# Weight splits and the attention half's additions to x move from GpSimd to VectorE in a two-layer hybrid encoder trunk

## The chip, the core and the metric

The kernel runs on one core of a Trainium2 chip. The metric is the time of one execution on the device in microseconds (us). A profile shows the engines of the core: PE (TensorE, matrix products; PEld is its weight load), DVE (VectorE), ACT (ScalarE), POOL (GpSimd) and SP, whose queue issues the DMA transfers. Engines work through their own instruction lists in order and wait for each other by semaphores.

## What is computed

x has 256 tokens of 1024 features. Two layers, each:

```
x += 1/2 SwiGLU_a(RMSNorm(x) * g)                    # D_FF = 2816
u  = (RMSNorm(x) * g) @ W_in                          # the mixer begins
     columns A: neighbourhood attention, 8 heads x 64
     columns B: short convolution, gates, long convolution (FFT), 512 channels
x += ([RMSNorm(y_A) ; RMSNorm(y_B)] * g_out) @ W_out  # the mixer ends
x += 1/2 SwiGLU_b(RMSNorm(x) * g)
x += sigmoid((RMSNorm(x) * g) @ W_g) * (p[i] @ W_p)
```

and a last RMSNorm. All arrays are float32. To keep more bits than one pass of the fast matrix format gives, each operand is split in two: `h`, the rounded copy, and `l`, what is left (`src - h`). A product is then the sum of three: h by h, h by l and l by h.

## The kernel before

All activations are kept transposed: feature on the partition, token (256) along the row, eight tiles `x[0..7]` of 128x256. Weights stream in from memory as pieces `raw` of 128x2048 (1 MB, three buffers). `part()` splits one half of a piece (eight tiles of 128x128, 128x1024 numbers) in two steps: ACT makes `wh` (a cast, L285), and then `wl = raw - wh` is one subtraction (L288). Six halves can be split ahead of use. The variable `Stream.on_pool` decides who does the subtraction: inside the mixer every third half goes to POOL (`ON_POOL = 3`), elsewhere all go to DVE. The last reader of a piece frees its buffer for the next load.

`Fiber`s are generators that are stepped while PE's matmuls are written out, and so they set where side work stands between the matmuls. PE's and ACT's instructions keep the order in which they are written. DVE's, POOL's and SP's are placed by the framework's scheduler.

The order in the mixer (`ORDER`): value columns, then groups of columns for gate (`g`), query and key (`q`), scores (`s`), transposes of the softmax (`t`), attention (`p`), transform of u (`u`, `f`), outer gate (`x`), inverse transform (`i`), and at the end `a0` to `a7`: the attention half of W_out's product, one 128x256 tile of x each. `add(c, ps, st, e)` waits for the row scale of the norm (`rna`), multiplies on DVE (L942) and adds to `x[c]` (L943) on the engine `e`, which is POOL here. Then comes the convolution half of the same product, whose row scale is `rhy`: it multiplies and adds on DVE (L942, L943), and at once `prep` makes the next stage's operand: ACT writes `xg` (L368), DVE its remainder (L370), ACT squares x (L353), POOL sums the squares in `acc` (L356). PE's first products of the next SwiGLU (L191, L200) read `xg`.

Other names in the rows: L426 to L435 are the small instructions of a norm's row scale (`Rstd`), L442 and L443 its broadcast on PE, L444 its copy; L731 to L742 make q and k; L839 and L840 are the side taps of the short convolution; L854 is the gate product `u` on POOL; L779 scales the softmax and L786 transposes it.

Of the kernel before, what the change touches and what calls it, by code (L numbers as in the profile page):

```python
# [49 lines left out]
SPREAD_F = 10  # L50
FILTER = 10
LAG = 0
ON_POOL = 3

# [24 lines left out]
def hybrid_trunk(ctx: ExitStack, tc: tile.TileContext, w, xT, pT, rpb, small, wf, zT, dft, idft, decay, out):  # L81
    nc = tc.nc
    V, S, G, PE = nc.vector, nc.scalar, nc.gpsimd, nc.tensor
# [15 lines left out]
    def nm(s):  # L99
        uid[0] += 1  # L100
        return f"{s}{uid[0]}"

    def bank():
        return psp.tile([P, 512], F32, tag="ps", name=nm("ps"))
# [4 lines left out]
    def t1(dt=F32, s="s"):  # L109
        return k1.tile([P, T], dt, tag="k1", name=nm(s))  # L110
# [4 lines left out]
    def f(ap):  # L115
        return ap.bitcast(F32)
# [31 lines left out]
    def spawn(gen, first=False):  # L148
        fb = Fiber(gen)
        Pace.live.insert(0 if first else len(Pace.live), fb)  # L150
        return fb
# [13 lines left out]
    def rest(n):  # L165
        for _ in range(n):
            yield

    def mm3(o, lh, ll, rh, rl, start, stop):
        PE.matmul(o, lh, rh, start=start, stop=False)  # L170
        PE.matmul(o, lh, rl, start=False, stop=False)  # L171
        PE.matmul(o, ll, rh, start=False, stop=stop)  # L172
        paced(o.free_size() // T if hasattr(o, "free_size") else o.shape[-1] // T)
# [66 lines left out]
    class Stream:  # L240
        loaded = 0
        parted = 0
        used = 0
        on_pool = 0
        raws = {}
        ready = {}

    def load():
        n = Stream.loaded
        if n >= DEPTH * PIECES:  # L250
            return
        raw = rawp.tile([P, 16, P], F32, tag="raw", name=nm("raw"))
        src = w[n].rearrange("p (a b) -> p a b", b=P)
        if n == 0:
            nc.sync.dma_start(sm, small)
            for q in range(4):
                nc.sync.dma_start(raw[:, 4 * q : 4 * q + 4], src[:, 4 * q : 4 * q + 4])
                nc.sync.dma_start(x[q], xT[q])
        elif n == 1:
            for q in range(2):  # L260
                nc.sync.dma_start(x[4 + 2 * q], xT[4 + 2 * q])
                nc.sync.dma_start(raw[:, q * HALF : (q + 1) * HALF], src[:, q * HALF : (q + 1) * HALF])
                nc.sync.dma_start(x[5 + 2 * q], xT[5 + 2 * q])
        else:
            nc.sync.dma_start(raw, src)
        Stream.raws[n] = raw
        Stream.loaded += 1

    def part(steps=1):

        n = Stream.parted
        Stream.parted += 1
        while Stream.loaded < min(n // 2 + 2, DEPTH * PIECES):
            load()
        raw = Stream.raws[n // 2]
        h = whp.tile([P, HALF, P], F32R, tag="wh", name=nm("wh"))
        l = wlp.tile([P, HALF, P], F32R, tag="wl", name=nm("wl"))
        fb = Fiber(None)
        Stream.ready[n] = (h, l, fb)

        def go():
            k = HALF // steps
            for a in range(0, HALF, k):
                src = raw[:, n % 2 * HALF + a : n % 2 * HALF + a + k]
                S.copy(h[:, a : a + k], src)  # L285
                yield
                e = G if Stream.on_pool and n % Stream.on_pool == 0 else V
                e.tensor_sub(l[:, a : a + k], src, f(h[:, a : a + k]))  # L288
            if n % 2:
                Stream.raws.pop(n // 2)  # L290
                load()

        fb.gen = go()
        return fb

    def half():

        n = Stream.used
        Stream.used += 1
        h, l, fb = Stream.ready.pop(n)  # L300
        fb.finish()
        refill(n - LAG)
        return h, l
# [40 lines left out]
    class Squares:  # L344
# [5 lines left out]
        def add(self, src):  # L350
            self.seen += 1
            q = self.ac if self.seen == 1 else t1(s="q")
            S.activation(q, src, AF.Square)  # L353
            last = self.seen == self.n
            if self.seen > 1 and (self.join or not last):
                G.tensor_add(self.ac, self.ac, q)  # L356
            if last:
                self.parts.extend([self.ac] if self.join else [self.ac, q])
# [308 lines left out]
    def mixer(i):  # L667
# [3 lines left out]
        def columns(between=None):  # L671

            b = bank()
            product(b[:, :T], ws, xs)
            if between:
                between()
            product(b[:, T:], ws, xs)
            return b
# [4 lines left out]
        for quarter in range(4):  # L683
            h, l = half()
# [59 lines left out]
        class Head:  # L744
# [7 lines left out]
            def scores(self, st):  # L752
                st.fb.finish()
                b = bank()
                for tt in range(2):
                    qs = slice(T * self.par + tt * P, T * self.par + (tt + 1) * P)
                    mm3(b[:, tt * T : (tt + 1) * T], st.qh[:, qs], st.ql[:, qs], st.kh, st.kl, True, True)
                self.e = t2()
                self.fb = spawn(self.softmax(b), True)
# [21 lines left out]
            def turn(self):  # L781
                self.fb.finish()
                b = bank()
                for kt in range(2):
                    for tt in range(2):
                        PE.transpose(  # L786
                            b[:, kt * T + tt * P : kt * T + (tt + 1) * P],
                            self.e[:, tt * T + kt * P : tt * T + (kt + 1) * P],
                            ident,
                        )  # L790
                self.h, self.l = t2(F32R), t2(F32R)
                self.fb = spawn(self.parts(b), True)
# [6 lines left out]
        yna, yhy = [], []  # L799
# [47 lines left out]
        def gated(c, b):  # L847
            t = t1(s="u")

            def go():  # L850
                res = [t1(), t1()]
                yield from conv(b, (8 + c, 4 + c), res)
                yield
                G.tensor_mul(t, *res)  # L854

            u.append((t, spawn(go())))
# [3 lines left out]
        def outer(c, b):  # L860
            res = [t1(s="x0"), t1(s="x0")]
            fb = spawn(conv(b, (c, c + 1), res))
            x0.extend((r, fb) for r in res)
# [65 lines left out]
        def project(wo, c, parts):  # L929
            ps = bank()[:, :T]  # L930
            for k in range(4):
                wh, wl = wo.next()
                hl, fb = parts[k]
                fb.finish()
                mm3(ps, wh, wl, hl[:, :T], hl[:, T:], k == 0, k == 3)
            return ps

        def add(c, ps, st, e):
            yield from rest(EV)
            yield from st.wait()  # L940
            t = t1()
            V.tensor_mul(t, ps, st.dst)  # L942
            e.tensor_add(x[c], x[c], t)  # L943
# [21 lines left out]
        qs, hs, added, wo = {}, {}, [], Tiles()  # L965
        for kind, j in MIXER:
            if kind == "g":
                gated(j, columns())
            elif kind == "q":
                qs[j] = QK(columns())  # L970
            elif kind == "x":
                outer(2 * j, columns())
            elif kind == "s":
                hs[j] = scores(j, qs.pop(j))
            elif kind == "t":
                turn(hs[j])
            elif kind == "p":
                attend(j, hs.pop(j))
                if len(yna) == 4:
                    na = Rstd(rna, nsq.parts, HY, [fb for _, fb in yna], STAT_NA, SPREAD_NA)  # L980
            elif kind == "u":
                u_turned()
            elif kind == "f":
                forward(j)
            elif kind == "i":
                backward(j)
                if len(yhy) == 4:
                    hy = Rstd(rhy, hsq.parts, HY, [fb for _, fb in yhy], STAT_HY, SPREAD_HY)
            elif kind == "a":
                added.append(spawn(add(j, project(wo, j, yna), na, G)))  # L990
        wo = Tiles()
        new_norm()
        for c in range(KD):
# [9 lines left out]
    def ple_input(i):  # L1003
        pr = t2()
        nc.sync.dma_start(v2(pr), pT[i].rearrange("(a p) t -> p a t", p=P))
        ph, pl = t2(F32R), t2(F32R)

        def go():
            yield from rest(8)
            split(pr, ph, pl)  # L1010

        return ph, pl, spawn(go())
# [88 lines left out]
        Pace.live.append(part())  # L1101
    scaled.extend((hl, Fiber(iter(()))) for hl in hls)
    for i in range(DEPTH):
        Stream.on_pool = 0
        flt = spawn(filter_steps(i))
        ffn(i, C_MIX, i)
        flt.finish()
        Stream.on_pool = ON_POOL
        mixer(i)
        Stream.on_pool = 0  # L1110
        given = ple_input(i)
        ffn(i, C_PLE, i)
        ends, outs = ple(i, i == DEPTH - 1, given)
# [146 lines left out]
```

## Time and profile before

| what | value |
|---|---|
| time, median of 3 runs | 1099.89 us (1099.7 to 1102.32) |
| profiled execution, its own time | 1098.94 us |
| its span, first to last instruction | 1097.2 us |
| PE busy | 1066.1 us (97%) |
| DVE busy | 912.0 us (83%) |
| ACT busy | 649.2 us (59%) |
| POOL busy | 266.1 us (24%) |
| splits of weights on DVE, on POOL (L288) | 328, 22 |
| additions L943 on DVE, on POOL | 16, 16 |
| mean granted clock of PE | 0.994 |

The mixers of the two layers lie at about 203 to 343 us and 732 to 881 us of the span. [...]

### The profile page before, as it was taken

What the parts mean: (1) busy time and instruction counts of PE and PEld (TensorE: products, weight loads), DVE (VectorE), ACT (ScalarE), POOL (GpSimd) and SP (SyncE); (2) the same over time, 40 slices, a digit from 0 to 9 for tenths busy, and PEclk for the clock granted to TensorE, in tenths of its full rate; (3) what the DMA queues carried; (4) which work ended last, traced back from release to release, by engine and by line L of the source; (5) the groups of instructions that cost most, each with busy time, mean ns of one, the idle gap of its engine ahead of it and who ended that gap; (6) DMA issues with size and microseconds to landing.
All of it is one profiled execution on the core that took longest, in us unless ns stands there. A gap on an engine that the chain in (4) does not pass through costs nothing.

```text
span 1097.2 us, 18014 instructions
## 1 busy us (share of the span) xinstructions
PE 1066.1 (97%) x6716; PEld 964.1 (88%) x6716; DVE 912.0 (83%) x1552; ACT 649.2 (59%) x1182; POOL 266.1 (24%) x270
## 2 busy tenths in 40 slices
PE   7989999999998999999999999999999999999995
PEld 6878888899997888888988888889989888888895
DVE  4999987798999988856789999787899998886565
ACT  7566565367746766554666665544856476665444
POOL 3211120534363211100112113025442721110101
PEclk9989999999999999999999999999999999999998
DMA  8556545554425555555465654554622465554621
GB/s 318 199 202 227 192 163 183 177 180 163 154 78 201 196 192 193 188 192 177 169 211 184 231 192 158 188 177 168 194 78 90 151 220 202 192 192 159 208 94 39
DMA packets 32983, 194.07 MB, mean 177 GB/s; under 512 B 3584, under 2 KB 6528, under 8 KB 10880
## 3 DMA queue, kind: packets, MB, share of 16 engines
q1 hardware_dynamic: 32896, 192.92, 51.4%
q8 instruction: 53, 0.87, 0.3%
q14 instruction: 34, 0.28, 0.1%
HBM read 191.86 MB, written 1.05 MB: 176 GB/s over the span
## 4 chain that ended last, share of the span: by engine, by line
PE 79%; DVE 13%; ACT 4%; issue 3%; DMA 0%; POOL 0%; SPq 0%; DVEq 0%; ACTq 0%; POOLq 0%
PE ps L191 41%; PE ps L200 21%; PE ps L171 5%; PE ps L172 5%; PE ps L170 5%; DVE wl L288 3%; ACT wh L285 1%; DVE s L839 1%; DVE rt L399 1%; DVE x L943 1%; DVE s L942 1%; ACT t L779 1%; DVE xg L370 1%; ACT t L772 0%; DVE y L808 0%
## 5 line engine op out<-in xcount | busy, mean ns | idle before, releaser
L288 DVE TENSOR_TENSOR wl<-raw,wh 128x1024 fp32r<-128x1024 f32 (+1 forms) x328 | 405.3, 1258 | 103.2 <-PE ps L200 61.3
L285 ACT CAST wh<-raw 128x1024 fp32r<-128x1024 f32 (+1 forms) x350 | 362.4, 1042 | 157.0 <-PE ps L191 86.1
L191 PE MATMUL ps<-xg,wh 128*128 128x512 f32 x1408 | 347.3, 396 | 12.9 <-DVE xg L1091 6.7
L191 PEld LDWEIGHTS ps<-xg,wh 128*128 128x128 f32 x1408 | 260.0, 191 | 64.7 <-DVE xg L370 8.1
L200 PEld LDWEIGHTS ps<-xg,wl 128*128 128x128 f32 x1408 | 182.1, 191 | 7.7
L200 PE MATMUL ps<-xg,wl 128*128 128x256 f32 x1408 | 184.2, 283 | 0.0
L191 PE MATMUL ps<-act,wh 128*128 128x512 f32 x704 | 173.0, 391 | 0.0
L490 POOL TENSOR_TENSOR gu<-gu,rb 128x256 f32<-128x256 f32 x88 | 69.6, 796 | 394.4 <-DVE gu L208 326.3
L191 PEld LDWEIGHTS ps<-act,wh 128*128 128x128 f32 x704 | 128.3, 189 | 23.9
L356 POOL TENSOR_TENSOR acc<-acc,q 128x256 f32<-128x256 f32 x62 | 55.9, 902 | 295.0 <-ACT q L353 293.8
L170 PE MATMUL ps<-xg,wh 128*128 128x256 f32 x448 | 127.5, 285 | 0.0
L171 PE MATMUL ps<-xg,wh 128*128 128x256 f32 x448 | 126.7, 283 | 0.0
L172 PE MATMUL ps<-xg,wl 128*128 128x256 f32 x448 | 126.7, 283 | 0.0
L200 PEld LDWEIGHTS ps<-act,wl 128*128 128x128 f32 x704 | 92.9, 191 | 5.1
L200 PE MATMUL ps<-act,wl 128*128 128x256 f32 x704 | 94.4, 282 | 0.0
L171 PEld LDWEIGHTS ps<-xg,wh 128*128 128x128 f32 x448 | 85.9, 192 | 0.1
L170 PEld LDWEIGHTS ps<-xg,wh 128*128 128x128 f32 x448 | 85.9, 192 | 0.1
L172 PEld LDWEIGHTS ps<-xg,wl 128*128 128x128 f32 x448 | 85.9, 192 | 0.0
L205 ACT COPY gu<-ps 128x256 f32<-128x256 f32 x176 | 56.2, 374 | 33.1 <-PE ps L200 32.7
L288 POOL TENSOR_TENSOR wl<-raw,wh 128x1024 fp32r<-128x1024 f32 x22 | 56.1, 2550 | 64.0 <-ACT wh L285 51.2
L208 DVE TENSOR_TENSOR gu<-gu,ps 128x256 f32<-128x256 f32 x176 | 66.3, 413 | 0.0
L368 ACT ACTIVATE xg<-x,sm 128x256 fp32r<-128x256 f32 x56 | 28.2, 508 | 59.3 <-DVE x L527 39.9
(196 smaller groups left out, 1386.9 us busy)
## 6 DMA issues: line engine op xcount, KB each, us to landing
raw<-in_w SPq DMA_DIRECT2D x172, 1024.0 KB, 5.0
bias<-in_rpb SPq DMA_DIRECT2D x16, 256.0 KB, 2.9
raw<-in_w SPq DMA_DIRECT2D x4, 256.0 KB, 4.4
x<-in_xT SPq DMA_DIRECT2D x8, 128.0 KB, 5.0
raw<-in_w SPq DMA_DIRECT2D x2, 512.0 KB, 5.5
t<-in_wf SPq DMA_DIRECT2D x4, 256.0 KB, 5.6
dec<-in_decay SPq DMA_DIRECT2D x4, 256.0 KB, 6.3
out<-o SPq DMA_DIRECT2D x4, 256.0 KB, 2.5
```

The lines of the kernel that those rows point to most:

```text
L170: PE.matmul(o, lh, rh, start=start, stop=False)
L171: PE.matmul(o, lh, rl, start=False, stop=False)
L172: PE.matmul(o, ll, rh, start=False, stop=stop)
L191: PE.matmul(b, lh, r, start=start, stop=False)
L200: PE.matmul(o, ll, rh, start=False, stop=stop)
L205: S.copy(dst, b[:, T:])
L208: V.tensor_add(dst, dst, b[:, :T])
L285: S.copy(h[:, a : a + k], src)
L288: e.tensor_sub(l[:, a : a + k], src, f(h[:, a : a + k]))
L356: G.tensor_add(self.ac, self.ac, q)
L368: S.activation(hl[:, :T], x[c], AF.Copy, scale=g)
L490: G.tensor_mul(u, u, rb)
```

## The change

All splits go to DVE, and so do the additions of the attention half to x. POOL's list in the two mixers loses 22 subtractions and 16 additions; DVE's gains the same 38. No instruction of PE, ACT or SP changes its place. DVE's list is placed by the scheduler, so some neighbours of the added rows trade places as well.

```
-ON_POOL = 3
...
-        on_pool = 0
...
                 S.copy(h[:, a : a + k], src)
                 yield
-                e = G if Stream.on_pool and n % Stream.on_pool == 0 else V
-                e.tensor_sub(l[:, a : a + k], src, f(h[:, a : a + k]))
+                V.tensor_sub(l[:, a : a + k], src, f(h[:, a : a + k]))
...
             elif kind == "a":
-                added.append(spawn(add(j, project(wo, j, yna), na, G)))
+                added.append(spawn(add(j, project(wo, j, yna), na, V)))
...
-        Stream.on_pool = 0
         flt = spawn(filter_steps(i))
         ffn(i, C_MIX, i)
         flt.finish()
-        Stream.on_pool = ON_POOL
         mixer(i)
-        Stream.on_pool = 0
```

Line numbers of the changed kernel are lower by three from the subtraction on (L288 is L285 there, L943 is L940).

DVE's list in the first layer's mixer, where the first gate's convolution ends (`s_2455`) and the first q and k (`t_2552`) are made, before:

```order
L839 SCALAR_TENSOR_TENSOR s_2455<-t_2470,sm,s_2455 128x255
L715 TENSOR_TENSOR vl_2353<-t_2474,vh_2349 128x2x64
L840 SCALAR_TENSOR_TENSOR s_2455<-t_2470,sm,s_2455 128x255
L715 TENSOR_TENSOR vl_2353<-t_2474,vh_2349 128x2x64
L731 TENSOR_TENSOR t_2552<-ps_2442,rb 128x512
```

The same place in the changed kernel:

```order
L285 TENSOR_TENSOR wl_2486<-raw_2325,wh_2485 128x1024
L836 SCALAR_TENSOR_TENSOR s_2455<-t_2470,sm,s_2455 128x255
L712 TENSOR_TENSOR vl_2353<-t_2474,vh_2349 128x2x64
L837 SCALAR_TENSOR_TENSOR s_2455<-t_2470,sm,s_2455 128x255
L712 TENSOR_TENSOR vl_2353<-t_2474,vh_2349 128x2x64
L728 TENSOR_TENSOR t_2552<-ps_2442,rb 128x512
```

The split `wl_2486`, which POOL did beside these rows, now stands ahead of them in DVE's own list.

DVE's list at the end of the first layer's mixer, from the attention half's products to the first instruction of the convolution half's row scale, before:

```order
L942 TENSOR_TENSOR s_3694<-ps_3653,rna_2364 128x256
L942 TENSOR_TENSOR s_3697<-ps_3625,rna_2364 128x256
L942 TENSOR_TENSOR s_3700<-ps_3605,rna_2364 128x256
L942 TENSOR_TENSOR s_3713<-ps_3670,rna_2364 128x256
L288 TENSOR_TENSOR wl_3690<-raw_3308,wh_3689 128x1024
L942 TENSOR_TENSOR s_3741<-ps_3688,rna_2364 128x256
L426 TENSOR_SCALAR v_3747<-ps_3744 128x2
```

And in the changed kernel:

```order
L285 TENSOR_TENSOR wl_3655<-raw_3308,wh_3654 128x1024
L939 TENSOR_TENSOR s_3694<-ps_3653,rna_2364 128x256
L939 TENSOR_TENSOR s_3697<-ps_3625,rna_2364 128x256
L940 TENSOR_TENSOR x_87<-x_87,s_3694 128x256
L940 TENSOR_TENSOR x_86<-x_86,s_3697 128x256
L939 TENSOR_TENSOR s_3700<-ps_3605,rna_2364 128x256
L939 TENSOR_TENSOR s_3713<-ps_3670,rna_2364 128x256
L940 TENSOR_TENSOR x_85<-x_85,s_3700 128x256
L940 TENSOR_TENSOR x_88<-x_88,s_3713 128x256
L285 TENSOR_TENSOR wl_3690<-raw_3308,wh_3689 128x1024
L939 TENSOR_TENSOR s_3741<-ps_3688,rna_2364 128x256
L423 TENSOR_SCALAR v_3747<-ps_3744 128x2
```

One split and four additions came in ahead of the row scale (`v_3747`); a fifth addition follows it directly.

More of the change, by code (lines that the diff above doesn't have):

```diff
@@ L52 @@
 LAG = 0
-ON_POOL = 3
 ORDER = "g0 q0 g1 s0 q1 g2 t0 s1 g3 q2 t1 p0 u0 q3 f0 s2 f1 p1 s3 t2 x0 x1 t3 i0 p2 p3 i1 i2 i3 a0 a1 a2 a3 a4 a5 a6 a7"
@@ L243, in hybrid_trunk @@
         used = 0
-        on_pool = 0
         raws = {}
@@ L286, in go @@
                 yield
-                e = G if Stream.on_pool and n % Stream.on_pool == 0 else V
-                e.tensor_sub(l[:, a : a + k], src, f(h[:, a : a + k]))
+                V.tensor_sub(l[:, a : a + k], src, f(h[:, a : a + k]))
             if n % 2:
@@ L989, in mixer @@
             elif kind == "a":
-                added.append(spawn(add(j, project(wo, j, yna), na, G)))
+                added.append(spawn(add(j, project(wo, j, yna), na, V)))
         wo = Tiles()
@@ L1103, in hybrid_trunk @@
     for i in range(DEPTH):
-        Stream.on_pool = 0
         flt = spawn(filter_steps(i))
@@ L1107, in hybrid_trunk @@
         flt.finish()
-        Stream.on_pool = ON_POOL
         mixer(i)
-        Stream.on_pool = 0
         given = ple_input(i)
```

## The prediction

> **What bounds the kernel now.** I read the page's shares first (the table above), then the busy times of the stretches around the change, then what PE waits for in them. Everything moved lies in the two mixers. I cut each in two, its middle and its end (the projections and the first `xg`):
>
> ```profile
> core 0: us, PE busy (x) PEld busy (x) DVE busy (x) ACT busy (x) POOL busy (x), PEclk, DMA share, GB/s
> 203.00:306.00 103.00, 101.59 (x758) 96.45 (x758) 88.94 (x152) 65.29 (x136) 42.50 (x38) 1.00 0.48 159
> 306.00:345.00 39.00, 35.69 (x265) 33.58 (x265) 37.62 (x82) 22.17 (x41) 25.35 (x21) 1.00 0.38 124
> 732.00:840.00 108.00, 105.88 (x783) 100.16 (x782) 93.36 (x155) 66.95 (x138) 45.53 (x40) 1.00 0.44 147
> 840.00:882.00 42.00, 39.14 (x288) 36.68 (x286) 40.70 (x84) 23.91 (x46) 26.21 (x21) 1.00 0.40 134
> ```
>
> PE hardly pauses, so whatever the change does must show as longer or shorter pauses of PE. DVE is busy 86% of the middles and 96 to 97% of the ends: in the middles it has some 14 us of slack each, at the ends almost none. DMA is under half busy, so the loads that the freed buffers start are not the limit. What PE waited for, first mixer and then second:
>
> ```profile
> PE ps L191 <- DVE xg L370: 3.3, 3, 1.9
> PE ps L170 <- ACT t L738: 0.6, 1, 0.6
> PE ps L171 <- DVE s L740: 0.3, 1, 0.3
> PE ps L882 <- POOL u L854: 0.2, 1, 0.2
> ```
> ```profile
> PE ps L191 <- DVE xg L370: 2.9, 3, 1.5
> PE ps L786 <- ACT t L779: 1.2, 1, 1.2
> PE ps L171 <- DVE s L740: 0.3, 1, 0.3
> PE ps L170 <- ACT t L738: 0.2, 1, 0.2
> PE ps L442 <- DVE s L435: 0.2, 1, 0.2
> ```
>
> Two thirds are waits for `xg` at the ends, the rest single pauses in the middles. No matmul waits for a weight split. Matmul records overlap, so I size the pauses by starts:
>
> ```profile
> 235.62 0.28 PE L171 MATMUL ps<-xg,wh 128*128 128x256 f32 x1
> 235.74 0.28 PE L172 MATMUL ps<-xg,wl 128*128 128x256 f32 x1
> ...
> 237.89 0.28 PE L170 MATMUL ps<-s,t 128*128 128x256 f32 x1
> ```
> ```profile
> 769.42 0.28 PE L172 MATMUL ps<-xg,wl 128*128 128x256 f32 x1
> ...
> 771.20 0.28 PE L170 MATMUL ps<-s,t 128*128 128x256 f32 x1
> ```
> ```profile
> 816.30 0.28 PE L172 MATMUL ps<-s,t 128*128 128x256 f32 x1
> 817.76 1.92 PE L786 MATMUL ps<-ident,t 128*128 128x128 f32 x8 [1.19 <-ACT t L779]
> ```
>
> The undisturbed step is 0.12 us. Four steps took 2.15 us from 235.74 (the scores of the first heads, waiting for q and k), so 1.67 us were lost; 1.78 us from 769.42, so 1.30 lost; one step took 1.46 us from 816.30, so 1.34 lost.
>
> **Why DVE is late there.** Rows of POOL and DVE at one time:
>
> ```profile
> 231.43 2.70 POOL L288 TENSOR_TENSOR wl<-raw,wh 128x1024 fp32r<-128x1024 f32 x1 [4.11 <-ACT wh L285]
> 231.79 2.62 DVE L839 SCALAR_TENSOR_TENSOR s<-t,sm,s 128x255 f32<-128x255 f32 x1
> ```
>
> The tap L839 ends at 234.41, 0.28 us after POOL's split has ended at 234.13. The groups' shortest, median and longest durations (ns) say how unusual that is:
>
> ```profile
> L839 DVE SCALAR_TENSOR_TENSOR s<-t,sm,s x16: 471/482/2624, 230.6 to 797.2; 128x255 f32<-128x255 f32 x16
> L942 DVE TENSOR_TENSOR s<-ps,rna x16: 407/412/420, 314.7 to 857.6; 128x256 f32<-128x256 f32 x16
> L288 DVE TENSOR_TENSOR wl<-raw,wh x328: 692/1219/3217, 5.6 to 1067.5; 128x1024 fp32r<-128x1024 f32 x162, 128x512 fp32r<-128x512 f32 x2
> L288 POOL TENSOR_TENSOR wl<-raw,wh x22: 2400/2442/3384, 214.2 to 870.3; 128x1024 fp32r<-128x1024 f32 x22
> L943 DVE TENSOR_TENSOR x<-x,s x16: 408/946/2656, 327.6 to 875.1; 128x256 f32<-128x256 f32 x16
> ```
>
> L942, with one operand in PSUM (`ps`), never varies; L839, L943 and L288, with both in SBUF, are at times held until POOL's instruction ends. So a POOL split takes DVE time as well, sometimes more than doing it there.
>
> **The change part by part.**
>
> *Added to DVE:* 22 splits by 1.22 us (median) and 16 additions by 0.41 us (shortest, unheld): 26.8 + 6.6 = 33.4 us, 16.7 per mixer.
>
> *Taken off DVE:* the time for which it was held by what moves. I took each DVE record that overlaps a moved POOL instruction less the usual duration of its form. There are 26, about 13 a mixer; the first, the last and three that are needed below:
>
> ```profile
> 214.51 3.22 DVE L288 TENSOR_TENSOR wl<-raw,wh 128x1024 fp32r<-128x1024 f32 x1 [0.66 <-ACT wh L285]
> ...
> 225.06 2.41 DVE L288 TENSOR_TENSOR wl<-raw,wh 128x1024 fp32r<-128x1024 f32 x1 [0.94 <-ACT wh L285]
> ...
> 748.21 3.11 DVE L391 TENSOR_SCALAR rt<-v 128x2 int32<-128x2 int32 x1
> ...
> 806.21 2.62 DVE L740 TENSOR_TENSOR s<-t,s 128x256 fp32r<-128x256 f32 x1
> ...
> 871.17 2.28 DVE L943 TENSOR_TENSOR x<-x,s 128x256 f32<-128x256 f32 x2
> ```
>
> The first was held 2.0 us (3.22 - 1.22), the last pair 1.46 (2.28 - 0.82). All together, as an estimate since some overlap two POOL instructions: about 15 us in the first mixer and 20 in the second, 35 in sum. DVE's load is thus about unchanged (33.4 against 35); what changes is where it stands.
>
> *The middles.* There are eight moved splits in each, so 9.8 us more for DVE, inside 14 us of slack; the holds taken off are about 10 us in the first middle and 14 in the second. Ahead of the first q and k, three splits come in (3.7 us) and the holds at 214.51, at 231.79 (2.62 - 0.48 = 2.1) and at 225.06 (1.2) go, 5.3 us: q and k come 1.6 us earlier, and the 1.67 us pause closes. In the second mixer three splits come in against more than that (at 748.21 a row of the norm's scale, hardly any work, was held almost 3 us), so the 1.30 us pause closes too. The pause at 817.76 has one hold of 2.2 us in its chain (806.21, by 0.42) and one new split of 1.2 us: 1.0 of its 1.34 us goes. The small waits for u and L435 (0.2 each, 0.35 by the starts, since a record covers 0.16 of a pause) go: POOL's u no longer stands behind splits, and L435 follows the row held at 748.21. What is late next is the attention's own ACT work, which moves with PE. Sum of the middles: 1.6 + 1.3 + 1.0 + 0.7 = 4.6 us.
>
> *The ends.* Three splits and eight additions come in per layer: 3.7 + 3.3 = 6.9 us on an engine with almost no slack. What goes, in the first layer:
>
> ```profile
> 316.07 2.09 DVE L288 TENSOR_TENSOR wl<-raw,wh 128x1024 fp32r<-128x1024 f32 x1
> ...
> 318.81 0.67 DVE L393 TENSOR_SCALAR rt<-rt 128x2 int32<-128x2 int32 x1
> ...
> 323.67 1.63 DVE L288 TENSOR_TENSOR wl<-raw,wh 128x1024 fp32r<-128x1024 f32 x1 [0.32 <-ACT wh L285]
> 325.57 1.42 DVE L288 TENSOR_TENSOR wl<-raw,wh 128x1024 fp32r<-128x1024 f32 x1 [0.26 <-ACT wh L285]
> ...
> 327.57 2.29 DVE L943 TENSOR_TENSOR x<-x,s 128x256 f32<-128x256 f32 x2
> ...
> 333.94 0.96 DVE L943 TENSOR_TENSOR x<-x,s 128x256 f32<-128x256 f32 x1
> ...
> 337.51 2.83 DVE L943 TENSOR_TENSOR x<-x,s 128x256 f32<-128x256 f32 x2
> ```
>
> Holds of 0.9, 0.5, 0.4, 0.2, 1.5 and 1.5 us (of the 2.0 at 337.51, 0.5 is by a sum of squares that stays, as the whole of 0.55 at 333.94 is): 5.0 us, and the two idle gaps, 0.6 us. Net 1.3 us more; records overlap the next by about 0.08 us, which takes 0.8 off for eleven instructions. I take 0.5 us per layer, 1.0 in both. The row scale `rhy` comes some 2 us later, since one split and four or five additions stand ahead of it, and ACT's casts queue behind its row; the first `xg` comes about 1 us later, the last ones earlier or at the old distance, as the two long holds ahead of them go. Bounds per layer: 1.5 us gained (the last `xg` sets the end and the whole 2.9 to 3.3 us of waits halves) to 2 us lost (the first sets it and the delay of `rhy` is handed through).
>
> *At no cost:* POOL's own shorter list, since only u was waited for; buffers of `raw` freed sooner, since no matmul waits for a load.
>
> *Sum:* 4.6 - 1.0 = 3.6 us. The profiled execution, 1098.94 us (1.7 outside its span), becomes 1095.3; it lies 0.95 below the median 1099.89, so against the median 1096.3.
>
> [...]
>
> **The rivals.**
>
> *Given back at the end (same).* The middles' gain only brings PE to the projections sooner, where DVE at 97% sets the pace; the two ends then cost 2 us each and eat 4.0 of the 4.6: 1099.3. For it: the first `xg` is delayed. Against: DVE's list at the end starts from a row that waits for PE, so it moves along.
>
> *Both shrink (faster).* The ends gain 1.5 us each: 1099.89 - 4.6 - 3.0 = 1092.3.
>
> *DVE becomes the bound (slower).* At the ends the holds don't go but change their cause: the eight sums of squares (0.55 us each, as at 333.94) and the gate products meet the added work. With 4 us of holds taken off per end instead of 5.0, an end costs 6.9 - 4 - 0.6 = 2.3 us and the middles' gain is just eaten: from there on it decides. With 2 us taken off, each end costs 4.3, 8.6 in all, less 4.6: 1104. With nothing taken off it would be 1108. Against: only sums of squares remain on POOL there, a few tenths each.
>
> **How the numbers follow.** About 0.3% (3.3 us) is what a measurement can tell from no change. The forecast, 1094 to 1098, has 0.50, of which 0.36 lies under 1096.6; both shrink 0.14; given back 0.24; slower 0.12. So faster 0.50, same 0.38, slower 0.12. The range reaches from the shrinking ends, 1091.5, to between the last two rivals, 1102.
>
> **What would show it.** POOL's rows L288 and L943 gone; L839's longest under 1.4 us; DVE busy within 5 us of 912; no pause over 0.3 us at the first scores. If the wait for `xg` grows beyond 5 us a layer, the ends were wrong; if the first scores still wait, the middles were. A DVE split of 1.2 us whose median rises would say that the holds have another cause.

## The result and the profile after

The changed kernel takes 1093.11 us (median of 4 runs, 1092.21 to 1093.29); the kernel before, in the same session, 1100.01 us (1099.7 to 1102.32). The ratio is 0.9934, with a 95% interval of 0.9919 to 0.9948: 0.66% or 6.9 us faster. The profiled executions show 1.2 us less of it: their spans are 1097.2 and 1091.5 us, since the one of before lies 1.07 below its median and that of the changed kernel 0.18 above.

The windows of the two middles and the two ends, in the changed kernel (busy us and number of rows of PE, PE's weight loads, DVE, ACT, POOL; then clock and DMA):

```profile
203.00:306.00 103.00, 102.86 (x785) 98.99 (x784) 90.49 (x172) 66.44 (x138) 23.83 (x31) 1.00 0.47 159
306.00:345.00 39.00, 36.03 (x257) 33.17 (x256) 38.62 (x83) 23.37 (x44) 8.71 (x9) 1.00 0.43 145
732.00:840.00 108.00, 107.72 (x821) 103.47 (x820) 95.02 (x183) 69.39 (x144) 26.07 (x32) 1.00 0.41 139
840.00:882.00 42.00, 39.54 (x268) 35.92 (x267) 40.89 (x94) 22.29 (x43) 10.73 (x9) 1.00 0.52 182
```

In the middles PE lacks 0.14 and 0.28 us of being always busy, where it lacked 1.41 and 2.12. POOL's time falls by 19 us per middle and DVE's rises by only 1.6, though it has 20 and 28 rows more (some of them come from the work of 3 us that the windows now hold beside). What PE still waits for, first mixer and then second, is at the ends alone, and one wait is new (L439, the broadcast of the convolution half's row scale):

```profile
PE ps L190 <- DVE xg L367: 2.5, 3, 1.2
PE ps L439 <- DVE s L432: 0.5, 1, 0.5
```
```profile
PE ps L190 <- DVE xg L367: 1.6, 3, 0.7
PE ps L439 <- DVE s L432: 0.8, 1, 0.8
```

The first scores in the timeline, where 1.67 us were lost before; now every start follows the last by 0.12 us:

```profile
234.66 0.28 PE L171 MATMUL ps<-xg,wl 128*128 128x256 f32 x1
234.78 0.28 PE L169 MATMUL ps<-s,t 128*128 128x256 f32 x1
...
235.15 0.28 PE L169 MATMUL ps<-s,t 128*128 128x256 f32 x1
```

The groups' shortest, median and longest durations (ns) in the changed kernel:

```profile
L285 DVE TENSOR_TENSOR wl<-raw,wh x350: 691/1218/2312, 5.2 to 1060.9; 128x1024 fp32r<-128x1024 f32 x173, 128x512 fp32r<-128x512 f32 x2
L836 DVE SCALAR_TENSOR_TENSOR s<-t,sm,s x16: 471/476/485, 227.0 to 790.4; 128x255 f32<-128x255 f32 x16
```

The tap, once held up to 2.62 us, never takes more than 0.485 in this form. The median of the 350 splits is where that of the 328 was.

**Where the 6.9 us came from.** PE's 6716 matmuls come in the same order in both kernels, so the n-th start of one can be set against the n-th of the other. How much earlier (-) or later (+) a stretch of the program ended than it began, in us, against the kernel before, for every run; beside it how long DVE was held in the same four stretches (each DVE record less the shortest tenth of its line and form, interpolated, and summed; at most 0.74 us of a stretch lies in rows that no POOL row overlaps). The stretches run from and to the same matmuls in every kernel, those at 203, 306, 345, 732, 840 and 882 us of the kernel before.

| kernel | middle 1 | end 1 | middle 2 | end 2 | held: middle 1, end 1, middle 2, end 2 |
|---|---|---|---|---|---|
| before | 0 | 0 | 0 | 0 | 12.1, 9.7, 15.1, 10.3 |
| changed (all) | -2.86 | +0.13 | -3.19 | +0.05 | 2.3, 5.2, 4.1, 4.9 |
| splits only | -2.86 | -0.21 | -3.20 | -0.27 | 2.4, 7.0, 4.3, 6.7 |
| additions only | -0.02 | +1.73 | -0.01 | +1.29 | 12.0, 9.5, 15.1, 9.4 |
| + POOL subtractions (run 3) | +7.55 | +6.70 | +4.61 | +5.54 | 14.8, 10.5, 15.1, 10.3 |
| + POOL memsets (run 4) | -2.66 | +0.14 | -3.19 | +0.46 | 4.1, 5.2, 4.9, 5.3 |
| middles' splits only | -2.88 | +0.40 | -3.19 | -0.02 | 2.4, 10.1, 4.1, 10.3 |
| splits, end's squares | -2.86 | -0.80 | -3.19 | -0.63 | 2.3, 3.8, 4.1, 3.7 |
| all, end's squares | -2.86 | -0.46 | -3.20 | -0.29 | 2.1, 1.9, 4.2, 2.1 |

The middles give 6.05 us, the ends take 0.18: 5.9 us, against 5.7 in the spans. The FFN stages between differ by at most 0.04. The kernel's start and last stage differ from before's by up to 1.2 and 0.9 us, without relation to the edit (of the start, part goes with the clock, which was low after a pause of 3.6 us at about 70 us in both: over 66 to 82 us it was 0.79 in the execution of before and 0.89 in that of the changed kernel). So these steps are sharper than the times. The other 1.0 us of the 6.9 is not traced to the edit; before's own executions in the next session ranged from 1097.19 us at a granted clock of 0.995 to 1102.42 at 0.989.

### The profile page after: what moved, and what is told of

The parts are those of the page before. It is cut to its first block, busy times and chain, and to the rows that moved or that the text cites. A ratio compares the mean times of both kernels' runs of the same rounds, so it can differ in the third digit from the quotient of the medians.

```text
span 1091.5 us, 17975 instructions
## 1 busy us (share of the span) xinstructions
PE 1064.5 (98%) x6716; PEld 964.0 (88%) x6716; DVE 912.1 (84%) x1590; ACT 649.4 (59%) x1182; POOL 196.2 (18%) x232
## 4 chain that ended last, share of the span: by engine, by line
PE 85%; DVE 10%; DMA 2%; ACT 2%; issue 1%; SPq 0%; ACTq 0%; DVEq 0%
PE ps L190 40%; PE ps L199 21%; PE ps L169 7%; PE ps L170 7%; PE ps L171 7%; DVE wl L285 3%; DMA raw<-in_w 2%; DVE x L940 1%; DVE s L939 1%; DVE rt L396 1%; DVE xg L367 1%; ACT wh L283 1%; PE ps L783 1%; DVE y L805 0%; PE ps L415 0%
## 5 line engine op out<-in xcount | busy, mean ns | idle before, releaser
L285 DVE TENSOR_TENSOR wl<-raw,wh 128x1024 fp32r<-128x1024 f32 (+1 forms) x350 | 427.6, 1244 | 98.4 <-PE ps L199 62.1
L494 DVE TENSOR_TENSOR s<-s,gu 128x256 f32<-128x256 f32 x88 | 55.0, 634 | 0.4 <-ACT s L491 0.2
```

Of the source, the lines that this page charges most:

```text
L285: V.tensor_sub(l[:, a : a + k], src, f(h[:, a : a + k]))
L494: V.tensor_mul(s, s, u)
```

## The experiments

My theory: the gain is DVE time and order won back from POOL's instructions that read SBUF, and it sits in the middles; the additions at the ends cost. The main rival: the gain comes from something else that goes with POOL's shorter list, as `raw` that comes free sooner, `u` that no longer stands behind splits, or simply a less busy POOL.

**1. Only the splits.** The changed kernel with the additions left on POOL:

```
-                added.append(spawn(add(j, project(wo, j, yna), na, V)))
+                added.append(spawn(add(j, project(wo, j, yna), na, G)))
```

> Splits on VectorE, the attention half's additions still on GpSimd. Theory (what GpSimd's splits cost is the time for which VectorE is held while GpSimd reads): the pauses in the two middles close as in the changed kernel, about 6 us, and the ends change by less than 1.5 us either way, since the additions on GpSimd hold VectorE for about 2 us per end but take 3.3 us off its list: 1092 to 1095 us. Rival (the additions carry the gain, since x no longer crosses engines): most of the gain is missing, 1097 to 1100 us.

1091.73 us (6 runs, 1090.48 to 1092.29), ratio 0.9931 (0.9917 to 0.9944) to 1099.66 of before; a little under the 1092 to 1095 expected. What PE waits for, first mixer, then second:

```profile
PE ps L190 <- DVE xg L367: 2.7, 3, 1.3
```
```profile
PE ps L190 <- DVE xg L367: 1.9, 3, 0.9
PE ps L439 <- DVE s L432: 0.2, 1, 0.2
```

The whole gain of the middles is there. The wait at L439 is gone or small, so it belongs to the additions. The times alone cannot part this kernel from the changed one (the intervals overlap); the table's ends do: 0.34 and 0.32 us better.

**2. Only the additions.** The kernel before with `V` for `G` in the same line.

> Additions on VectorE, every third split of the mixers still on GpSimd. Theory: the middles stay as before, and each end gets 3.3 us of additions while the three splits there still hold VectorE: no gain, 1099 to 1102 us. Rival (the additions carry the gain): 1094 to 1097 us.

1101.66 us (12 runs), ratio 1.0019 (1.0009 to 1.003): slower. The middles are untouched, to 0.02 us; the ends lose 1.73 and 1.29. The waits of PE at the ends, first mixer, then second:

```profile
PE ps L191 <- DVE xg L370: 3.7, 2, 1.9
...
PE ps L442 <- DVE s L435: 0.5, 1, 0.5
```
```profile
PE ps L191 <- DVE xg L370: 2.5, 3, 1.2
PE ps L442 <- DVE s L435: 1.4, 2, 1.2
```

The additions bring 3.3 us per end to DVE, and take off only 0.2 and 0.9 us of holds (table: 9.7 to 9.5, 10.3 to 9.4), since the added rows are now held too: at 315.58 two of them took 2.29 us beside a POOL split.

**3. A POOL instruction that reads, put back.** The changed kernel, and in the mixers, after each third split on DVE, POOL does another subtraction of the split's size into `raw`, which nobody reads. No row of PE, ACT or DVE moves:

```
                 V.tensor_sub(l[:, a : a + k], src, f(h[:, a : a + k]))
+                if Stream.extra and n % 3 == 0:
+                    G.tensor_sub(src, src, f(h[:, a : a + k]))
```

> The changed kernel, and after every third split in the mixers GpSimd subtracts once more, raw - wh written over raw, which nobody reads again: VectorE's list is word for word that of the changed kernel, and GpSimd is busy as long as before, some 2.4 us 22 times. It only adds work that nobody waits for, but for the raw buffer, which is freed 2.4 us later. Theory (holding): the holds of about 30 us come back on top of the 33 us that VectorE took over, and the ends, which have no slack, pass on most of what falls there: 1100 to 1112 us. Rival (the gain is that a split takes 1.2 us in place of 2.4 and that GpSimd's list is free for u): within 1 us of the changed kernel for the splits, at most 2 us for u: 1093 to 1095 us.

1122.8 us (4 runs), ratio 1.0214 (1.0197 to 1.023): 29.7 us slower than the changed kernel, and 10.8 beyond the top of the range that I had thought of. POOL's and DVE's timelines at the first scores:

```profile
233.64 2.75 POOL L288 TENSOR_TENSOR raw<-raw,wh 128x1024 f32<-128x1024 f32 x1 [4.63 <-DVE wl L286]
```
```profile
234.08 2.59 DVE L840 SCALAR_TENSOR_TENSOR s<-t,sm,s 128x255 f32<-128x255 f32 x1
```

The tap is held to 2.59 us again, by an instruction that nothing depends on. What PE waited for from the first mixer's start on (the largest rows):

```profile
PE ps L190 <- DVE xg L370: 4.7, 2, 3.0
PE ps L169 <- ACT t L738: 2.8, 1, 2.8
PE ps L882 <- POOL u L854: 2.8, 1, 2.8
PE ps L442 <- DVE s L435: 2.6, 2, 2.1
```

Why it cost more: the holds of all four stretches are about those of before (table), but here DVE carries the splits and the additions beside them; it is busy 946.0 us instead of 912.1. The wait for `u` is a hold as well: the tap L840 that it reads was held to 2.51 us (at 266.35), and POOL stood idle for 1.34 us before `u` began. One other part: after some of the long pauses PE ran slower (last section), worth 5.2 us in the first mixer. Which part has how much was not separated.

**4. A POOL instruction that only writes, at the same places.** Two memsets of the same tile instead:

```
+                    G.memset(src, 0.0)
+                    G.memset(src, 0.0)
```

> As the run with the extra subtraction, at the same places and with the same waits, but GpSimd only writes: two memsets of raw, about 1 us each. Theory (VectorE is held by GpSimd instructions that read): within 1 us of the changed kernel, 1092.5 to 1094.5 us, and no VectorE row longer than about 1.4 us in the middles. Rival (any GpSimd work there, or the later release of raw, costs the time): as the extra subtraction, 1100 us or more.

1093.7 us (4 runs), ratio 0.9943 (0.9924 to 0.9963): the changed kernel's time. Its middles by windows, and POOL and DVE at one time in its timeline:

```profile
203.00:306.00 103.00, 102.86 (x783) 98.86 (x782) 91.12 (x171) 66.18 (x138) 40.25 (x47) 1.00 0.47 159
...
732.00:840.00 108.00, 107.72 (x821) 103.47 (x820) 95.65 (x182) 69.26 (x144) 41.32 (x48) 1.00 0.41 140
```
```profile
230.65 0.95 POOL L288 MEMSET raw<- 128x1024 f32 x1 [3.76 <-DVE wl L286]
```
```profile
231.10 0.48 DVE L841 SCALAR_TENSOR_TENSOR s<-t,sm,s 128x255 f32<-128x255 f32 x1
```

POOL is about as busy as in the kernel before (40.25 against 42.50, 41.32 against 45.53), `raw` comes free late again, and `u` again has work ahead of it; PE's busy time in the middles is to the digit that of the changed kernel. By the starts 0.6 us are lost against it: 0.2 in the first middle, at `u`, which now starts right behind the second memset, and 0.4 at an `xg` of the second end. The tap that starts inside a memset takes its 0.48 us. So POOL's load, the buffers and its queue make 0.6 us at most, and the rest goes with the subtraction, which reads SBUF where the memset only writes it: the tap took 2.59 us beside the one in run 3 and 0.48 beside the other here.

**5. Only the middles' splits.** The kernel before, with POOL keeping the three splits of each end:

```
-                e = G if Stream.on_pool and n % Stream.on_pool == 0 else V
+                e = G if n in (96, 99, 102, 270, 273, 276) else V
```

> Only the eight splits in each mixer's middle go to VectorE; the three splits and the eight additions at each end stay on GpSimd. If the middles carry the gain and the ends give nothing (what the alignment of the matmuls says of the version with all splits moved, 0.25 us per end), the time is that version's, 1091.7 us, to within 1 us. If the prediction's own account of the ends holds (a moved split adds 1.22 us to a VectorE with no slack, and the three take only 2.0 us of holds off), leaving them on GpSimd is worth 1.7 us an end: about 1088.5. If the end's splits were held more than that, it is slower than 1091.7 by 2 us or more.

1093.72 us (5 runs), ratio 0.9955 (0.9942 to 0.9967), beside a before of 1098.49. The middles' gain is all there; the ends are 0.61 and 0.25 us worse than with all splits moved. The waits for `xg`, first mixer, then second, are about those of before (3.3 and 2.9):

```profile
PE ps L191 <- DVE xg L370: 3.7, 3, 1.9
```
```profile
PE ps L191 <- DVE xg L370: 2.9, 3, 1.5
```

So the prediction's account of the splits at the ends, 3.7 us in and 2.0 out, would have made this the fastest kernel, and it was not: moving those three splits took 3.1 and 3.6 us of holds off (10.1 to 7.0, 10.3 to 6.7). That only about balances the 3.7 us that they bring, so what gives PE the 0.61 and 0.25 us was not shown.

**6. Splits, and the end's sums of squares.** POOL's seven additions per mixer for the next norm go to DVE too (`new_norm(e=V)` at the mixer's end); the attention half's additions stay on POOL:

```
-                G.tensor_add(self.ac, self.ac, q)
+                self.e.tensor_add(self.ac, self.ac, q)
```

> Splits on VectorE, additions on GpSimd as in the version at 1091.7 us, and the seven additions of squares at the mixer's end (L353, the sums for the next norm) on VectorE as well. They held VectorE for 5.4 to 5.8 us in each mixer by the after trace; on VectorE they cost 7 x 0.41 = 2.9 us per end. If holds are what an end pays for GpSimd's work, each end gains up to 2.5 us and the waits for xg shrink from 2.7 and 1.9 us: 1088 to 1090.5. If the last waits for xg do not hang on VectorE's load, or the new work in VectorE's order waits for ScalarE's squares, it stays within 1 us of 1091.7 or gets slower.

1090.56 us (5 runs, 1089.28 to 1092.49), ratio 0.9926 (0.9914 to 0.9938). The fastest median of all, and by times alone not to be told from the splits only; by the table its ends are 0.59 and 0.36 us better than there, less than the 2.5 that I had put as the most. The seven additions took 3.2 and 3.0 us of holds off and cost 7 x 0.42 = 2.9. Its waits at the ends:

```profile
PE ps L190 <- DVE xg L368: 2.4, 2, 1.3
```
```profile
PE ps L190 <- DVE xg L368: 1.2, 2, 0.9
PE ps L440 <- DVE s L433: 0.2, 1, 0.2
```

**7. Both, and the additions.** The changed kernel with the sums of squares on DVE.

> The changed kernel (splits and additions on VectorE) with the seven additions of squares at each mixer's end on VectorE too, so that only the gating product of the next stage (L487) is left on GpSimd there. VectorE then carries 3.3 us of additions more than the run before this one and no hold by them. By the holds: additions on GpSimd held VectorE for about 1.9 us an end and cost 3.3 there, so this is 1 to 3 us slower than the version with the squares alone moved, and 0 to 4 us faster than the changed kernel's 1093.1. If additions on VectorE cost only because they met the sums of squares on GpSimd, the two are equal.

1092.17 us (5 runs), ratio 0.9939 (0.9925 to 0.9952). Only 1.9 and 2.1 us of holds are left at the ends, and yet they are 0.34 us each worse than in run 6 (by the times 1.6 us in all, where 1 to 3 was expected). The wait for the row scale is back, in the first mixer and in the second:

```profile
PE ps L440 <- DVE s L433: 0.5, 1, 0.5
```
```profile
PE ps L440 <- DVE s L433: 0.8, 1, 0.8
```

So with the splits on DVE the additions' price there is about 0.34 per end with the sums of squares on either engine (changed against run 1: 0.34 and 0.32), and it goes with their place ahead of the row scale, not with holds: by the starts each of the four ends loses 0.61 to 0.63 us at the broadcast of that row scale and gets 0.27 to 0.29 back at `xg`.

## Why the prediction was right, and where its steps were off

The forecast was 1096.3 in a range of 1091.5 to 1102, faster with 0.50; it is faster, at 1093.1. That lies just below the likeliest case's own 1094 to 1098, near the number of the rival "both shrink" (1092.3), but not for that rival's reason: the ends did not shrink. A gain of 3.6 us was forecast and 6.9 measured: the small pauses gave some 1.4 more, the ends 0.8 more, and 1.0 is the part of the medians that is not traced to the edit.

*DVE's load unchanged.* Right: 33.4 us in against 35 out was said, and DVE is busy 912.1 us after 912.0. The table's holds fall by 30.7 us (47.2 to 16.5), and 33.4 less 38 overlaps of 0.08 is 30.4. The 35 was too much in the second middle: 14 us of holds were said to go there, and 11.0 went (15.1 to 4.1).

*The large pauses of the middles.* Right in place and size. By the starts of the same matmuls the first scores of the first mixer gained 1.66 (1.6 was said), those of the second 1.29 (1.3), the softmax's transposes 1.07 (1.0). One hold was read too large: of the 2.95 us at 748.21 the moved split can have only 2.0, since it ended at 750.37; the row ended at 751.32, with two memsets (to 751.30) that stay on POOL, and in the changed kernel the same row is still held, to 0.89 us (at 744.79).

*The small pauses: the term that was mis-sized.* 0.7 us stood for `u` and the row scale L435 of the second mixer, the two that the waits listed. They gave 0.47 and 0.55. Three more pauses, too short for that list, closed too: the row scale's broadcast in the first mixer 0.41, and the last attention products of each mixer (300.81 and 835.08) 0.36 and 0.30. Together 2.1 instead of 0.7, which is nearly all of the difference between 6.05 and 4.6.

The reason given for `u` was wrong, too: it did not stand behind POOL's splits. In the kernel before:

```profile
262.63 1.49 DVE L839 SCALAR_TENSOR_TENSOR s<-t,sm,s 128x255 f32<-128x255 f32 x1 [2.63 <-ACT s L833]
```
```profile
265.70 1.58 POOL L854 TENSOR_TENSOR u<-s,s 128x256 f32<-128x256 f32 x1 [1.86 <-DVE s L840]
```

POOL had been idle for 1.86 us when `u` began. It waited for the last of four taps on DVE, the first of which had been held for 1.0 us (1.49 in place of 0.48). So this pause, too, came from a hold.

*The ends.* A loss of 0.5 each was said; 0.13 and 0.05 were lost. The sum was small for two errors that met. The splits cost nothing but gained (runs 1 and 5: 0.61 and 0.25 us), as they had held 3.1 and 3.6 us and not the 2.0 that I counted. The additions cost 0.34 and 0.32 us; they had held less than the 3.0 counted, 1.8 us (7.0 to 5.2, 6.7 to 4.9). The sums of squares that stay on POOL are seven per mixer, not eight. `rhy` did come later: its first product stands at 325.97 us and stood at 326.91, 0.9 us earlier while PE was 3.5 ahead, so 2.6 later against PE (2 was said). What I did not follow through is that PE itself waits for that row scale, in the broadcast. DVE's timeline, and then PE's, in the changed kernel:

```profile
315.43 1.21 DVE L285 TENSOR_TENSOR wl<-raw,wh 128x1024 fp32r<-128x1024 f32 x1
316.57 0.41 DVE L939 TENSOR_TENSOR s<-ps,rna 128x256 f32<-128x256 f32 x1
316.90 0.14 DVE L423 TENSOR_SCALAR v<-ps 128x2 f32<-128x2 f32 x1
...
320.10 0.47 DVE L432 TENSOR_SCALAR s<-ident,rh 128x128 fp32r<-128x128 f32 x2
```
```profile
320.63 0.38 PE L439 MATMUL ps<-s,ones 128*128 128x256 f32 x1 [0.51 <-DVE s L432]
```

By the matmuls' starts this costs 0.98 us in the first mixer and 1.32 in the second, and the waits for `xg` give back 0.92 and 1.24. That is the start of the rival "given back at the end", but `xg` made nearly all of it good. "DVE becomes the bound" did not come about: 4.5 and 5.4 us of holds went at the ends (table: 9.7 to 5.2, 10.3 to 4.9), where 5.0 was said and 4 was the point from which it decides.

*At no cost.* POOL's shorter list and earlier `raw`: run 4 undid both and lost 0.6 us of some 6, so that was right but for 0.2 us at `u` and 0.4 at the second end.

*Which engine for which work.* The 22 splits were better on DVE (run 1 against its before, 1091.73 against 1099.66 us), the 16 additions on POOL: by the ends run 1 is better than the changed kernel by 0.34 and 0.32 us, run 6 than run 7 by 0.34 each, and before than run 2 by 1.73 and 1.29.

## What to carry to other kernels

Work given to POOL had its price on DVE here: 22 splits, 26.8 us of work on DVE, had held it for 26.8 (47.2 to 20.4 in the table, before to splits only). So list the rows of the one engine that ran long while the other worked, and sum their excess, before calling the other's work free. When DVE is the late one, look at its order beside its load: DVE was busy as long after the change (912.1 us) as before (912.0), and the gain came where the held rows were ones that PE waits for; and a few small additions put ahead of a row scale cost PE 0.6 us at its broadcast here, although DVE's holds fell. Size a gain by the starts of all matmuls in the stretch, since a list of waits leaves out short pauses: three that it left out here gave 1.1 of 6 us.

## What had not been expected of the hardware

*PE's clock after a pause.* In run 3 PE was granted a lower clock after some of the pauses of 2 to 3 us: 0.97, 0.96 and 0.89 in windows of the first mixer where the changed kernel has 1.00. PE's timeline after the wait for `u`:

```profile
271.54 1.34 PE L882 MATMUL ps<-ident,u 128*128 128x128 f32 x5 [2.76 <-POOL u L854]
...
273.32 0.41 PE L169 MATMUL ps<-xg,wh 128*128 128x256 f32 x1
273.53 0.41 PE L170 MATMUL ps<-xg,wh 128*128 128x256 f32 x1
...
274.81 0.31 PE L170 MATMUL ps<-xg,wh 128*128 128x256 f32 x1
274.96 0.28 PE L171 MATMUL ps<-xg,wl 128*128 128x256 f32 x1
```

The 128x256 matmuls start 0.21 us apart instead of 0.12 until 274.81, 3.3 us after the pause. The clock by windows in run 3, first mixer and then second:

```profile
240.00:306.00 66.00, 63.10 (x491) 61.40 (x490) 60.70 (x93) 45.45 (x98) 25.06 (x19) 0.97 0.45 150
306.00:345.00 39.00, 34.22 (x261) 33.20 (x260) 38.24 (x91) 16.57 (x34) 10.27 (x8) 0.96 0.28 96
345.00:360.00 15.00, 12.00 (x61) 10.23 (x61) 15.00 (x19) 10.02 (x18) 7.16 (x8) 0.89 0.47 157
```
```profile
732.00:840.00 108.00, 103.77 (x718) 96.57 (x717) 98.62 (x146) 60.04 (x121) 48.75 (x39) 0.98 0.43 147
840.00:882.00 42.00, 38.71 (x308) 37.95 (x307) 40.43 (x91) 21.29 (x42) 10.16 (x8) 0.96 0.31 101
```

The missing shares make 66 x 0.03 + 39 x 0.04 + 15 x 0.11 = 5.2 us in the first mixer, and 108 x 0.02 + 42 x 0.04 = 3.8 us in the second. The length of a pause does not decide by itself: after one of 2.06 us (before 332.21) the matmuls were soon 0.21 us apart, from 332.88 on; after one of 2.82 us (before 238.27) they were 0.12 apart from 239.55 on. What else decides is open here. In the changed kernel's mixers PE's longest wait is 1.2 us, and their windows show a clock of 1.00.

*How much a hold can cost a tiny row.* In the kernel before, a 128x2 row of the norm's scale took 3.11 us beside a POOL split and two memsets behind it (748.21, L391). Where nothing holds it, the same line, three numbers lower in the changed kernel, takes:

```profile
317.36 0.16 DVE L388 TENSOR_SCALAR rt<-v 128x2 int32<-128x2 int32 x1
```

That is 2.95 us of DVE for 256 elements, and the row has a single tensor input, where the held taps, splits and additions have two. Run 4 shows that such rows are held by memsets as well. Two of them on POOL, and these rows on DVE:

```profile
744.84 0.95 POOL L288 MEMSET raw<- 128x1024 f32 x1
745.84 0.95 POOL L289 MEMSET raw<- 128x1024 f32 x1
```
```profile
744.96 0.85 DVE L392 TENSOR_SCALAR rt<-v 128x2 int32<-128x2 int32 x1
745.03 0.78 DVE L393 TENSOR_SCALAR rt<-v 128x2 f32<-128x2 f32 x1
745.84 0.97 DVE L394 TENSOR_SCALAR rt<-rt 128x2 int32<-128x2 int32 x1
```

They end at 745.81 and 746.81, with the two memsets (745.79 and 746.79). So "a POOL instruction that only writes holds nothing" is true in run 4 of the taps (0.48 us) and splits (1.22 us, as at 214.62 beside a memset from 214.69 on), not of these; here a hold was 0.6 to 0.8 us, and PE did not wait for it. The changed kernel has the like from memsets of its own (the 0.89 us at 744.79). Why memsets hold these rows and not the taps was not shown.
